# A decoder block with 32 experts: the overflow loop after the third group of experts, the first dispatch by token blocks, and one prefetch page fewer

## The chip, the cores and the metric

The kernel runs on one core of a Trainium2 chip. The time is that of the device for one execution, in microseconds (us). Three executions of the kernel before took 1099.38, 1103.64 and 1104.58; the median is 1103.64. The profile is of one more execution. The engines are TensorE (PE, with its weight loads PEld), VectorE (DVE), ScalarE (ACT), GpSimd (POOL) and SyncE (SP), which issues nearly all loads.

## The reference

The input is 512 tokens of 1024 channels. Cut to what matters here:

```python
u = rms_norm(h)
proj = u @ w_in                               # z | xBC | dt | glu_a | glu_b | two gates
y_ssd  = rms_norm(ssd(conv4(xBC)) * silu(z)) @ w_ssd_out
y_conv = silu(layer_norm(causal_dwconv31(glu_a * sigmoid(glu_b)))) @ w_conf_out
h = h + (sigmoid(gate_ssd) * y_ssd + sigmoid(gate_conv) * y_conv) @ w_o
u = rms_norm(h)
# hierarchical MoE: the best of 4 groups, then the 2 best of its 8 experts
for each expert e:                            # 32 experts, D_EXPERT = 512
    xb = the tokens that chose e
    h[those tokens] += gate * ((silu(xb @ w_gate[e]) * (xb @ w_up[e])) @ w_down[e])
h = h + (p @ w_ple_proj) * sigmoid(rms_norm(h) @ w_ple_gate)
out = rms_norm(h)
```

All values are float32. An expert has 6 MB of weights.

## The kernel before, in words

Products in the mixers and the epilogue split each float32 operand into two parts of a faster type: a high part (a cast on ACT, line 302) and the remainder (a subtraction on DVE), and multiply high by high, high by low and low by high. The names `uh` and `ul` are such halves of the activations, and `w` that of a weight.

All work is a list `units`. A unit has weight loads and a function that issues its matmuls. `step()` takes the next one: it splits the weights of the units ahead (`split`), issues loads (`pump`, line 282, on SP), runs the unit's matmuls and then what was attached to that unit: a `job` belongs to a fixed unit, while a `task` has a first and a last unit between which a credit of PE time lets it go. All weights go into a pool of `PAGES` = 11 tiles of 1 MB, tag `w`; a mixer weight takes half of one. `state["room"]` counts the half pages that may be filled, and `free(n)` adds to it. One page's place is taken in the MoE by the one-hot tables, so ten are left.

Ahead of the MoE, `mixer` units of the two branches, `w_o`, and the router follow each other. `XD` is the unit by which the SSD products are done, `NB` the first unit of the MoE. In the mixers the layer norm sums `k` tiles (ACT, line 929) with a matmul by `ones`.

The MoE has seven groups, counted from 0 here and in what follows, of 4, 5, 5, 5, 5, 5 and 3 experts. The tokens of an expert are put into slots of 32 by a one-hot matmul (`disp`, four accumulators of 16 matmuls, each with a high part `u2h` and a low part `u2l` of the activations, whose tiles are `uh` and `ul` in the traces, and a copy to `cj`). Two quads of slots then pass six units each: gate and up in two halves of the depth (`eg`, `eu`), and two of down (`ed`), 32 matmuls a unit. The result is scaled by the gate weight in two parts (the last on DVE, `bt`), and `combine` adds it to `h` (`Z` in the traces) with the transposed one-hot tables: eight steps of four matmuls and a DVE addition. The combine of a group and the dispatch of the one after the next stand as tasks among the units of a group.

An expert with more tokens than its slots is served by the overflow loop, lines 1704 and 1705: `n_ext` (tile `cd`) is loaded into a register by every engine, and the body runs so often. With these inputs it is zero. Before, the loop stands behind all seven groups and ahead of the epilogue, whose transposes (`ident`, `Z`) need the finished `h`.

Of the kernel before, what the change touches and what calls it, by code (L numbers as in the profile page):

```python
# [19 lines left out]
NT = T // 128  # L20
KD = D // 128
# [46 lines left out]

_CST = {}
PAGES = 11  # L70
BT = dict(room=8, raw=20, hi=1, page=1.27, mm=3.5, cap=5.0, sp=5, fill=[1.8, 0.9], late=[7, 2])


# [63 lines left out]
def tile_hybrid(ctx: ExitStack, tc: tile.TileContext, x, p, chan, rowv, rows, cst, w_in, w_ssd, w_conf, w_o,  # L137
# [8 lines left out]
    def st(shape, dt, tag, bufs=1):  # L146
        return sb.tile(shape, dt, name=tag, tag=tag, bufs=bufs)
# [7 lines left out]
    def mm(o, a, b, start, stop):  # L155
        nc.tensor.matmul(o, a, b, start=start, stop=stop)
        if b.dtype == F32:
            nc.pe[0] += max(0.1, 3 * o.shape[-1] / 2370)
# [67 lines left out]
    def page(shape, dt, key):  # L226
# [3 lines left out]
        if v is None:  # L230
            v = st([128, 4 * T], dt, "w", PAGES)
            pend[key] = v[:, 2 * T:]
# [23 lines left out]
    def unit(src, mms, cost=0.0, plain=False):  # L256
        srcs = [] if src is None else src if isinstance(src, list) else [src]
        units.append(dict(lds=[load(s, plain) for s in srcs], mms=mms, cost=cost, plain=plain))
        return len(units) - 1

    def job(n, f, *a):
        jobs[n].append((f, a))
# [4 lines left out]
    def task(early, late, cost, f, *a):  # L267
        tasks.append((early, late, cost, f, a))

    def pump():  # L270
        while state["load"] < len(loads):
# [4 lines left out]
            if ld["wide"]:  # L276
                state["room"] -= 2
                ld["t"] = st([128] + list(src.shape[1:]), F32, "w", PAGES)
            else:
# [8 lines left out]
    def split_hi():  # L288
        n = state["split"]
        if n >= len(units):  # L290
            return False
        u = units[n]
        if u["lds"] and not u["plain"]:
            ld = u["lds"][0]
            if "t" not in ld:
                pump()
            if "t" not in ld:
                assert n >= NB
                return False
            u["raw"] = ld["t"]  # L300
            u["wh"], u["wl"] = [page(list(u["raw"].shape), F32R, n) for _ in range(2)]
            nc.scalar.copy(u["wh"], u["raw"])  # L302
        state["split"] += 1
        return True

    def split_lo():
        n = state["lo"]
        if n >= state["split"]:
            return
        state["lo"] += 1  # L310
        u = units[n]
        if u["lds"] and not u["plain"]:
            nc.vector.tensor_sub(u["wl"], u["raw"], u["wh"])
            free(1)

    def split():
        split_hi()
        split_lo()
# [22 lines left out]
    def after(u):  # L341
# [3 lines left out]
        state["n"] = n + 1  # L345
        state["credit"] = min(state["credit"] + BT["page"] * (2 if u["plain"] else 1) * len(u["lds"]) - u["cost"], BT["cap"])
        while True:
# [7 lines left out]
    def step():  # L355
        n = state["n"]
        top = state["top"]
        if n < NB:
            while state["split"] <= min(max(n + 2, 2 * n - NB + BT["sp"]), top):
                split()  # L360
        else:
            while state["split"] <= min(top, n + (BT["hi"] if n < NC else 6)) and split_hi():
                split_lo()
        pump()
        u = units[n]
        if u["plain"]:
            ws = [ld["t"] for ld in u["lds"]]
            u["mms"](ws)
            free(2 * len(ws))
        elif u["mms"] is not None:  # L370
            u["mms"](u["wh"], u["wl"])
        after(u)

    def run(upto=None):
        while state["n"] < (len(units) if upto is None else upto):
            step()
# [517 lines left out]
    n = 0  # L894
# [11 lines left out]
    for c in range(NT):  # L906
        js.extend(chunk(c, f0 + c * TUNE["stride"]))
    XD = math.ceil(max(j[0] for j in js if j[1] in (ssd_diag, ssd_skip)))
    job(XD + 1, free, 2)
    if TUNE["first"]:  # L910
        step_jobs(js)
    for w in seq:
# [96 lines left out]
    conv_out(0)  # L1009
    job(conv_out(1), free, BT["room"] - 6)  # L1010

# [47 lines left out]
    job(NO, load_h)  # L1059
    NB = len(units)  # L1060
    for i in range(4, 0, -1):
        job(NB - i, free, 2 if i > 1 else BT["raw"] - BT["room"] - 8)

    def add_h(c, n):
        hv = hh_["h"][:, c, n * 512:(n + 1) * 512]
# [3 lines left out]
    R = {}  # L1069
# [105 lines left out]
    G = {}  # L1175

    def weights(w, b):

        if b < NFIX:
            v = w[b]  # L1180
        else:
            if b not in G:
                G[b] = nc.sync.value_load(R["eid"][0:1, b:b + 1], min_val=0, max_val=NEXP - 1)
            v = w[bass.ds(G[b], 1)].rearrange("o a n -> (o a) n")
        return v.rearrange("(p k) n -> p k n", p=128)
# [5 lines left out]
    GW = {gi: QS * len(g) for gi, g in enumerate(GROUPS)}  # L1191
# [8 lines left out]
    def gu_unit(gi, q, i, kp):  # L1200
        quad = GROUPS[gi][q]

        def mms(ws):
            if kp == 0:
                PG[gi, q, i] = acc()
            for kk in range(4):
                k = 4 * kp + kk
                strips(PG[gi, q, i], XT[gi, k // 2][:, k % 2, q * QS:(q + 1) * QS], [w[:, kk, :] for w in ws], quad,
                       k == 0, k == KD - 1)
        return unit([lambda b=m[0]: weights((eg, eu)[i], b)[:, 4 * kp:4 * kp + 4, :] for m in quad], mms, BT["mm"],  # L1210
                    True)
# [32 lines left out]
    def one_hot(gi):  # L1244
        if gi == 0:
            G["ohs"] = st([128, 2, NT, 2 * QS], F32R, "w", PAGES)
        return G["ohs"][:, gi % 2]
# [19 lines left out]
    def disp_mm(gi, kp, pt, a):  # L1267
        w = GW[gi]
        for kk in range(2):
            k = 2 * kp + kk  # L1270
            for c in range(NT):
                mm(pt[:, kk * w:(kk + 1) * w], R[("u2h", "u2l")[a]][:, c, k * 128:(k + 1) * 128],
                   G["oh", gi][:, c, :w], a == 0 and kk == 0 and c == 0, a == 1 and kk == 1 and c == NT - 1)
# [7 lines left out]
    def disp(gi, kp):  # L1281
        pt = acc()
        for a in range(2):
            disp_mm(gi, kp, pt, a)
        disp_out(gi, kp, pt)
# [50 lines left out]
        fill_pe(state["n"], room)  # L1336

    combined = NB + 4
    for gi, g in enumerate(GROUPS):
        last = gi == len(GROUPS) - 1  # L1340
        first = len(units)
        if last:
            for n in range(2):
                p_unit(n)
            job(first - 6, free, -2)
            job(first - 5, p_load)
            job(first - 5, free, -2)
            for k in range(2):
                job(first - 3 + k, p_tr, k)
            job(first - 2, free, 2)  # L1350
            job(first - 2, free, -8)
        for q in range(len(g)):
            for kp in range(2):
                for i in range(2):
                    u = gu_unit(gi, q, i, kp)
            job(u - 1, hid_act, gi, q)
            job(u, hid_mul, gi, q)
            job(u, fill_now, BT["fill"][0])
            job(u, hid_tr, gi, q)
            job(u, fill_now, BT["fill"][1])  # L1360
            if last:
                job(u - 1, free, -2)
            for f in range(2):
                u = d_unit(gi, q, f)
            task(combined, u - 1, 1.4, back, gi, q)
            if last:
                job(u - 1, free, -2)
            for n in range(2):
                job(u, y_hi, gi, q, n)
                job(u, y_lo, gi, q, n)  # L1370
        if last:
            for n in range(2):
                for c in range(NT):
                    job(u, combine, gi, c, n)
            continue
        for n in range(2):
            for c in range(NT):
                task(u + 1, u + 5, 0.23 * 2 * len(g), combine, gi, c, n)
        combined = u + 5
        o = first + (BT["late"][0] if gi == 0 else BT["late"][1])  # L1380
        for q in range(len(GROUPS[gi + 1])):
            job(o, hot, gi + 1, q)
        for kp in range(4):
            task(o + 1, u, 0.115 * 16, disp, gi + 1, kp)
    for i in range(3):
        unit(None, None)
    NC = len(units)
# [144 lines left out]
    def u2_lo(n, c):  # L1532
        t = R.pop(("g", c, n)).rearrange("t (k p) -> t k p", k=KD)
        nc.vector.scalar_tensor_tensor(half(R["u2l"], c, n), t, rs[:, c:c + 1], half(R["u2h"], c, n),
                                       op0=OP.mult, op1=OP.subtract)
# [44 lines left out]
    for c in range(NT):  # L1580
        o = pp[:, c * NEXP:(c + 1) * NEXP]
# [7 lines left out]
    for c in range(NT):  # L1589
        hot_first(c)  # L1590
    for i in range(2 * NT):
        u2_lo(i // NT, i % NT)
    N2 = 2 * NEXP


# [93 lines left out]
    for i, f in enumerate((order0, order4, order1, order2, order3, order5, order6, order7, order8)):  # L1689
        job(NB + (i + 1) // 2, f)  # L1690
    pts = [acc() for _ in range(4)]
    for a in range(2):
        for k in range(4):
            disp_mm(0, k, pts[k], a)
    for k in range(4):
        disp_out(0, k, pts[k])
        if k % 2:
            step()
            step()
    run(NC)  # L1700

    W32 = [128, NEXP]
    ext, ntot, icnt, eidf, pos, gat = (R[n] for n in ("ext", "ntot", "icnt", "eidf", "pos", "gat"))
# [1 line left out]
    with tc.For_i(0, n_ext):  # L1705
# [39 lines left out]
        oh = st([128, NT, SL], F32R, "m", 2)  # L1745
# [38 lines left out]
        for w in (eg, eu):  # L1784
            o = acc()
            for q in range(4):
                for kk, (wh, wl) in enumerate(piece(w, [128, 2, DE], 2 * q)):
                    k = 2 * q + kk
                    a = xt[:, k].rearrange("p h a s -> p (h a s)")
# [36 lines left out]
                nc.vector.tensor_add(hv, hv, po)  # L1826
        nc.vector.tensor_scalar(icnt, icnt, 1.0, None, op0=OP.add)
    banks.remove(bank)
    if dbg == "moe":
        for c in range(NT):  # L1830
            nc.sync.dma_start(out[c * 128:(c + 1) * 128, :], h[:, c, :])
        return
# [77 lines left out]
```

## Time and profile before

| | us |
|---|---|
| median of three executions | 1103.64 |
| the profiled execution, its own time | 1103.84 |
| its span | 1102.1 |
| PE busy | 1017.3 |
| DVE busy | 561.7 |
| ACT busy | 344.7 |

The mean granted clock of TensorE is 0.978. The span runs from the first instruction to the last; the execution's own time is 1.7 us longer. A start time in the rows below is counted from the start of the span. A busy PE need not be PE at its peak.

### The profile page before, as it was taken

The numbers are of one execution on the slowest core, as the hardware profiler recorded it, in microseconds if no ns is written. First come the engines' busy times: TensorE is split into PE (matmuls) and PEld (weight loads), VectorE is DVE, ScalarE is ACT, GpSimd is POOL, SyncE is SP. The second block draws the span as 40 slices with busy tenths as digits, with TensorE's granted clock in tenths as the row PEclk, the third lists the DMA queues.
The fourth block names the chain that finished last, engine by engine and source line by source line (L and its number), as shares of the span: only waits on it lengthen the run. The fifth ranks groups of instructions, "written<-read, shape, count | busy, mean of one in ns | idle before, by whom it ended". The sixth has DMA issues, their size and how long they took to land. (4 is left out here: it accounts for less than half of the span.)

```text
span 1102.1 us, 15676 instructions
## 1 busy us (share of the span) xinstructions
PE 1017.3 (92%) x6262; PEld 673.0 (61%) x6262; DVE 561.7 (51%) x1004; ACT 344.7 (31%) x646; POOL 14.7 (1%) x32
## 2 busy tenths in 40 slices
PE   5999999999989999999799998989979979889796
PEld 4788889877767877788634453433514415345385
DVE  6689998897889955563721311202103002022365
ACT  5433446766443234432411010100100100121263
POOL 1000000000000000000000000000000000000010
PEclk9999999999999999999899999999999999999899
DMA  9323222201422323356189999999999999998701
GB/s 267 95 70 102 89 78 77 77 1 41 113 77 82 110 77 115 109 195 224 40 350 388 372 387 422 420 421 421 420 421 420 420 421 421 417 401 367 284 2 76
DMA packets 95660, 255.97 MB, mean 232 GB/s; under 512 B 4784, under 2 KB 62144, under 8 KB 71008
## 3 DMA queue, kind: packets, MB, share of 16 engines
q1 hardware_dynamic: 94896, 252.73, 60.6%
q0 software_dynamic: 688, 2.22, 0.7%
q8 instruction: 50, 0.82, 0.3%
q14 instruction: 26, 0.21, 0.1%
HBM read 252.83 MB, written 2.10 MB: 231 GB/s over the span
## 5 line engine op out<-in xcount | busy, mean ns | idle before, releaser
L120 PE MATMUL acc<-uh,w 128*128 128x512 f32 x704 | 231.0, 401 | 1.7 <-DVE w L120 1.6
L120 PE MATMUL acc<-w,cj 128*32 128x512 f32 x1664 | 200.3, 599 | 13.6 <-DMA w<-eu 9.9
L120 PE MATMUL acc<-w,uh 128*128 128x256 f32 (+2 forms) x752 | 161.7, 325 | 0.9 <-DVE w L120 0.9
L120 PEld LDWEIGHTS acc<-uh,w 128*128 128x128 f32 x704 | 132.2, 188 | 32.7 <-DVE w L120 2.6
L120 PE MATMUL acc<-w,m 128*32 128x512 f32 (+1 forms) x960 | 132.3, 595 | 19.2 <-DMA w<-ed 14.5
L120 PEld LDWEIGHTS acc<-w,cj 128*32 128x32 f32 x1664 | 54.4, 110 | 137.4 <-issue 106.6
L120 PE MATMUL acc<-ul,w 128*128 128x512 f32 x352 | 137.2, 390 | 0.0
L120 DVE SCALAR_TENSOR_TENSOR cj<-glu,chan,cj 128x512 f32<-128x512 f32 x180 | 130.8, 747 | 2.2
L120 PEld LDWEIGHTS acc<-w,uh 128*128 128x128 f32 x752 | 118.4, 193 | 21.0 <-issue 10.2
L120 DVE TENSOR_TENSOR w<-w 128x1024 fp32r<-128x1024 f32 x86 | 104.6, 1221 | 43.4 <-ACT w L302 43.2
L120 PE MATMUL acc<-w,ul 128*128 128x256 f32 (+2 forms) x488 | 117.2, 307 | 0.0
L302 ACT CAST w<-w 128x1024 fp32r<-128x1024 f32 x86 | 89.6, 1052 | 67.5 <-PE acc L120 54.4
L120 PE MATMUL acc<-w 128*128 128x512 f32 x384 | 102.0, 404 | 3.1 <-ACT w L302 2.4
L120 PEld LDWEIGHTS acc<-w,m 128*32 128x32 f32 (+1 forms) x960 | 44.5, 127 | 91.2 <-issue 53.1
L120 DVE TENSOR_TENSOR k<-k,acc 128x512 f32<-128x512 f32 x21 | 19.2, 913 | 151.4 <-PE acc L120 151.4
L120 PEld LDWEIGHTS acc<-w 128*128 128x128 f32 x384 | 73.9, 194 | 22.2 <-ACT w L302 2.8
L120 DVE TENSOR_TENSOR Z<-Z,acc 128x512 f32<-128x512 f32 x64 | 43.3, 686 | 85.1 <-PE acc L120 85.1
L120 PEld LDWEIGHTS acc<-w,ul 128*128 128x128 f32 x488 | 77.2, 189 | 5.6
L120 PEld LDWEIGHTS acc<-ul,w 128*128 128x128 f32 x352 | 66.2, 188 | 15.1 <-issue 1.7
L1227 ACT ACTIVATE k<-acc 128x512 f32<-128x512 f32 x13 | 7.8, 597 | 160.9 <-PE acc L120 160.9
L120 DVE SCALAR_TENSOR_TENSOR bt<-glu,chan,bt 128x512 f32<-128x512 f32 x60 | 43.0, 748 | 0.7
L120 DVE SCALAR_TENSOR_TENSOR bt<-acc,gt,k 128x512 fp32r<-128x512 f32 x12 | 9.0, 751 | 66.8 <-ACT k L1311 66.1
(270 smaller groups left out, 885.6 us busy)
## 6 DMA issues: line engine op xcount, KB each, us to landing
w<-eg SPq DMA_DIRECT2D x64, 1024.0 KB, 13.7
w<-eu SPq DMA_DIRECT2D x64, 1024.0 KB, 14.8
w<-ed SPq DMA_DIRECT2D x64, 1024.0 KB, 15.1
w<-w_in SPq DMA_DIRECT2D x52, 512.0 KB, 5.1
w<-w_ssd_out SPq DMA_DIRECT2D x8, 512.0 KB, 5.3
w<-w_conf_out SPq DMA_DIRECT2D x8, 512.0 KB, 4.3
w<-w_o SPq DMA_DIRECT2D x8, 512.0 KB, 4.8
w<-w_ple_gate SPq DMA_DIRECT2D x8, 512.0 KB, 13.3
```

What stands on the lines that cost most here:

```text
L120: return f(*a, **k)
L302: nc.scalar.copy(u["wh"], u["raw"])
L1227: nc.scalar.activation(t, PG.pop((gi, q, 0)), AF.Silu)
```

## The change

There are three parts.

1. `LG = 3`. The units run up to the first unit of group 3, and the overflow loop stands there. The combine of group 2 becomes a job of that group's last unit. The dispatch of group 3 is no longer a task among group 2's units; it is issued behind the loop, four accumulators in a row, and then the remaining units run.
2. In the first dispatch (group 0) the low part goes token block by token block (`c` outside, `k` inside) instead of accumulator by accumulator, and the low halves are written in the same order.
3. The two half pages that were given to the pool one unit behind `XD` are given to it with the last ones, one unit ahead of `NB`.

```diff
--- before.py
+++ after.py
@@ -68,6 +68,8 @@
 
 _CST = {}
 PAGES = 11
+
+LG = 3
 BT = dict(room=8, raw=20, hi=1, page=1.27, mm=3.5, cap=5.0, sp=5, fill=[1.8, 0.9], late=[7, 2])
 
 
@@ -906,7 +908,6 @@
     for c in range(NT):
         js.extend(chunk(c, f0 + c * TUNE["stride"]))
     XD = math.ceil(max(j[0] for j in js if j[1] in (ssd_diag, ssd_skip)))
-    job(XD + 1, free, 2)
     if TUNE["first"]:
         step_jobs(js)
     for w in seq:
@@ -1059,7 +1060,7 @@
     job(NO, load_h)
     NB = len(units)
     for i in range(4, 0, -1):
-        job(NB - i, free, 2 if i > 1 else BT["raw"] - BT["room"] - 8)
+        job(NB - i, free, 2 if i > 1 else BT["raw"] - BT["room"] - 6)
 
     def add_h(c, n):
         hv = hh_["h"][:, c, n * 512:(n + 1) * 512]
@@ -1336,9 +1337,12 @@
         fill_pe(state["n"], room)
 
     combined = NB + 4
+    NL = None
     for gi, g in enumerate(GROUPS):
         last = gi == len(GROUPS) - 1
         first = len(units)
+        if gi == LG:
+            NL = first
         if last:
             for n in range(2):
                 p_unit(n)
@@ -1375,13 +1379,17 @@
             continue
         for n in range(2):
             for c in range(NT):
+                if gi == LG - 1:
+                    job(u, combine, gi, c, n)
+                    continue
                 task(u + 1, u + 5, 0.23 * 2 * len(g), combine, gi, c, n)
         combined = u + 5
         o = first + (BT["late"][0] if gi == 0 else BT["late"][1])
         for q in range(len(GROUPS[gi + 1])):
             job(o, hot, gi + 1, q)
         for kp in range(4):
-            task(o + 1, u, 0.115 * 16, disp, gi + 1, kp)
+            if gi != LG - 1:
+                task(o + 1, u, 0.115 * 16, disp, gi + 1, kp)
     for i in range(3):
         unit(None, None)
     NC = len(units)
@@ -1589,7 +1597,7 @@
     for c in range(NT):
         hot_first(c)
     for i in range(2 * NT):
-        u2_lo(i // NT, i % NT)
+        u2_lo(i % 2, i // 2)
     N2 = 2 * NEXP
 
 
@@ -1689,15 +1697,19 @@
     for i, f in enumerate((order0, order4, order1, order2, order3, order5, order6, order7, order8)):
         job(NB + (i + 1) // 2, f)
     pts = [acc() for _ in range(4)]
-    for a in range(2):
-        for k in range(4):
-            disp_mm(0, k, pts[k], a)
+    for k in range(4):
+        disp_mm(0, k, pts[k], 0)
+    w = GW[0]
+    for c in range(NT):
+        for k in range(KD):
+            mm(pts[k // 2][:, k % 2 * w:(k % 2 + 1) * w], R["u2l"][:, c, k * 128:(k + 1) * 128], G["oh", 0][:, c, :w],
+               False, c == NT - 1 and k % 2 == 1)
     for k in range(4):
         disp_out(0, k, pts[k])
         if k % 2:
             step()
             step()
-    run(NC)
+    run(NL)
 
     W32 = [128, NEXP]
     ext, ntot, icnt, eidf, pos, gat = (R[n] for n in ("ext", "ntot", "icnt", "eidf", "pos", "gat"))
@@ -1826,6 +1838,9 @@
                 nc.vector.tensor_add(hv, hv, po)
         nc.vector.tensor_scalar(icnt, icnt, 1.0, None, op0=OP.add)
     banks.remove(bank)
+    for kp in range(4):
+        disp(LG, kp)
+    run(NC)
     if dbg == "moe":
         for c in range(NT):
             nc.sync.dma_start(out[c * 128:(c + 1) * 128, :], h[:, c, :])
```

On ACT, in the mixer, the rows show the cast of a weight among the `L929` activations (`k` tiles of the layer norm). Before:

```order
L929 ACTIVATE k_3318<-cj 128x512 [waits DVE_49]
L929 ACTIVATE k_3321<-bt 128x512 [waits DVE_49,PE_49,Activation_49]
L302 CAST w<-w 128x1024 [waits DMAHW7_49,PE_49]
L929 ACTIVATE k_3350<-cj 128x512 [waits DVE_49,Activation_49]
L302 CAST w<-w 128x1024 [waits DMAHW0_49,Activation_49]
L929 ACTIVATE k_3400<-bt 128x512 [waits DVE_49]
```

And in the changed kernel, the same six:

```order
L930 ACTIVATE k_3315<-cj 128x512 [waits DVE_49]
L930 ACTIVATE k_3318<-bt 128x512 [waits DVE_49,PE_49,Activation_49]
L304 CAST w<-w 128x1024 [waits DMAHW7_49]
L930 ACTIVATE k_3347<-cj 128x512 [waits DVE_49,PE_49,Activation_49]
L304 CAST w<-w 128x1024 [waits DMAHW0_49,Activation_49]
L930 ACTIVATE k_3397<-bt 128x512 [waits DVE_49,PE_49]
```

The order of the rows stays. The cast of the third row waits for a DMA and for PE before, and for the DMA alone after.

On SP, the rows ahead of the loop before stand at the end of the MoE: the loads of `w_ple_gate`, the load of the loop's count `cd`, and the branches past the loop.

```order
L282 DMA w<-w_ple_gate 128x2x512 [waits DMAHW3_49]
L282 DMA w<-w_ple_gate 128x2x512 [waits DMAHW4_49,PE_49]
L1704 TENSOR_LOAD cd [waits DVE_49]
L1704 ISA x2
L1705 COMPARE_AND_BRANCH
L1705 UNCONDITIONAL_BRANCH [waits SP_sequencer_49,DMAHW0_49,DMAHW1_49,DMAHW2_49,DMAHW3_49,DMAHW4_49,DMAHW5_49,DMAHW6_49,DMAHW7_49]
```

In the changed kernel the same branches stand behind the loads of group 3's first pages (`eg`, `eu`):

```order
L284 DMA w<-eg 128x2048 [waits DMAHW5_49,PE_49]
L284 ISA
L284 DMA w<-eu 128x2048 [waits DMAHW6_49,PE_49]
L1716 TENSOR_LOAD cd [waits DVE_49]
L1716 ISA x2
L1717 COMPARE_AND_BRANCH
L1717 UNCONDITIONAL_BRANCH [waits SP_sequencer_49,DMAHW0_49,DMAHW1_49,DMAHW2_49,DMAHW3_49,DMAHW4_49,DMAHW5_49,DMAHW6_49,DMAHW7_49]
```

Behind the loop's body, SP's next rows are these:

```order
L284 DMA w<-eu 128x2048
L284 ISA
L284 DMA w<-ed 128x2048
L284 ISA
L284 DMA w<-ed 128x2048
L284 ISA
L284 DMA w<-ed 128x2048 [waits PE_49]
```

The loop has moved among the loads of `eu` and `ed`: seven pages of group 3 are issued ahead of it. Of the loads behind it, three wait for nothing, and the fourth waits for PE.

On PE, before, the dispatch of group 3 (`w,uh` and `w,ul` into `acc`) stands among the units of group 2 (`w,cj` and `w,m`); four of its eight rows, and the units around them:

```order
L120 MATMUL acc<-cb,w 128x32 x8
L120 MATMUL acc<-w,cj 32x512 x16
L120 MATMUL acc<-w,uh 128x256 x8
L120 MATMUL acc<-w,ul 128x256 x8
L120 MATMUL acc<-w,uh 128x256 x8
L120 MATMUL acc<-w,ul 128x256 x8
L120 MATMUL acc<-w,cj 32x512 x48
```

In the changed kernel PE has the loop's branches behind the last matmuls of combine (`bt,glu`):

```order
L122 MATMUL acc<-k_5751,glu 128x512
L122 MATMUL acc<-bt,glu 128x512
L1716 TENSOR_LOAD cd
L1717 COMPARE_AND_BRANCH
L1717 UNCONDITIONAL_BRANCH x2
```

And behind the loop's body:

```order
L1717 UNCONDITIONAL_BRANCH
L122 MATMUL acc<-w,uh 128x256 x8
L122 MATMUL acc<-w,ul 128x256 x8
L122 MATMUL acc<-w,uh 128x256 x8
L122 MATMUL acc<-w,ul 128x256 x8
L122 MATMUL acc<-w,uh 128x256 x8
L122 MATMUL acc<-w,ul 128x256 x8
L122 MATMUL acc<-w,uh 128x256 x8
L122 MATMUL acc<-w,ul 128x256 x8
L122 MATMUL acc<-w,cj 32x512 x64
```

The dispatch's 64 matmuls of group 3 have moved out of group 2 and stand between the loop and the first units of group 3, `w,cj` x64.

## Rows read from the trace of the kernel before

**Rows 1.** The page, part 1: busy us (share of span), instructions

```profile
PE 1017.3 (92%) x6262; PEld 673.0 (61%) x6262; DVE 561.7 (51%) x1004; ACT 344.7 (31%) x646; POOL 14.7 (1%) x32
```

**Rows 2.** Windows, group 3: busy (count) per engine, PEclk, DMA share, GB/s

```profile
754.98:829.99 75.01, 67.90 (x517) 29.52 (x514) 13.20 (x27) 8.42 (x14) 0.00 (x0) 0.98 1.01 421
```

**Rows 3.** Waits of PE from 620 to 1030: us in total, times, longest

```profile
PE acc L120 <- DMA w<-ed: 14.5, 13, 2.3
```

**Rows 4.** Timeline of ACT, 403 to 422: start, us, instruction [idle <-releaser]

```profile
404.41 0.63 ACT L929 ACTIVATE k<-bt 128x512 f32<-128x512 f32 x1 [0.32 <-ACT k L929]
410.10 1.04 ACT L302 CAST w<-w 128x1024 fp32r<-128x1024 f32 x1 [5.06 <-PE acc L120]
```

**Rows 5.** The page, part 5: the casts

```profile
L302 ACT CAST w<-w 128x1024 fp32r<-128x1024 f32 x86 | 89.6, 1052 | 67.5 <-PE acc L120 54.4
```

**Rows 6.** Timeline of PE, 403 to 422

```profile
407.61 0.62 PE L120 MATMUL acc<-uh,w 128*128 128x512 f32 x2
408.07 0.39 PE L120 MATMUL acc<-ul,w 128*128 128x512 f32 x1
...
413.78 1.05 PE L120 MATMUL acc<-ones,k 128*128 128x1 f32 x8 [2.93 <-ACT k L929]
414.69 4.59 PE L120 MATMUL acc<-w 128*128 128x512 f32 x12
```

**Rows 7.** Windows in the stretch of rows 6, columns as in rows 2

```profile
414.00:420.00 6.00, 6.00 (x29) 5.06 (x28) 1.83 (x2) 2.46 (x4) 0.00 (x0) 0.72 0.00 0
```

**Rows 8.** Timeline of PE, then of DVE, first dispatch

```profile
538.42 0.45 PE L120 MATMUL acc<-dtx 128*128 128x32 bf16 x10 [5.62 <-DVE dtx L120]
539.80 6.36 PE L120 MATMUL acc<-w,uh 128*128 128x256 f32 x32 [0.93 <-DVE w L120]
545.99 3.79 PE L120 MATMUL acc<-w,ul 128*128 128x256 f32 x32
...
540.57 5.38 DVE L120 SCALAR_TENSOR_TENSOR ul<-cj,rst,uh 128x512 fp32r<-128x512 f32 x8
```

**Rows 9.** Waits of SP's queue, 1015 to 1043; windows there

```profile
SPq L1705 <- SPq L1705: 9.2, 5, 4.0
...
1037.00:1038.00 1.00, 1.00 (x6) 0.84 (x5) 1.00 (x3) 0.00 (x0) 0.00 (x0) 1.00 0.11 43
```

**Rows 10.** Timeline of PE, end of group 2 and start of group 3

```profile
750.09 4.56 PE L120 MATMUL acc<-w,m 128*32 128x512 f32 x25 [1.44 <-DMA w<-ed]
...
764.40 3.64 PE L120 MATMUL acc<-w,cj 128*32 128x512 f32 x32
```

**Rows 11.** Timeline of DVE, end of group 2 and the combine

```profile
754.98 1.61 DVE L120 SCALAR_TENSOR_TENSOR bt<-acc,gt,k 128x512 fp32r<-128x512 f32 x2 [15.02 <-ACT k L1311]
759.85 0.69 DVE L120 TENSOR_TENSOR Z<-Z,acc 128x512 f32<-128x512 f32 x1 [3.26 <-PE acc L120]
760.79 0.69 DVE L120 TENSOR_TENSOR Z<-Z,acc 128x512 f32<-128x512 f32 x1 [0.25 <-PE acc L120]
```

**Rows 12.** Timeline of SP where the stream restarts; windows there

```profile
553.38 0.80 SPq L282 DMA_DIRECT2D w<-ed  x2
...
554.20:554.60 0.40, 0.40 (x8) 0.13 (x4) 0.33 (x3) 0.00 (x0) 0.00 (x0) 1.00 1.72 246
```

**Rows 13.** Timelines of PE and DVE at the loop's exit; a window there

```profile
1042.42 3.15 PE L120 MATMUL acc<-ident,Z 128*128 128x128 f32 x16 [3.53 <-DVEq L1705]
...
1047.01 0.40 PE L120 MATMUL acc<-w,ul 128*128 128x512 f32 x1
...
1035.91 4.86 DVE L120 TENSOR_TENSOR Z<-Z,acc 128x512 f32<-128x512 f32 x8
1040.69 1.22 DVE L120 TENSOR_TENSOR w<-w 128x1024 fp32r<-128x1024 f32 x1
...
1045.91 0.74 DVE L120 SCALAR_TENSOR_TENSOR ul<-acc,chan,uh 128x512 fp32r<-128x512 f32 x1
...
1043.00:1044.00 1.00, 1.00 (x7) 1.00 (x6) 0.06 (x1) 0.89 (x2) 0.31 (x1) 0.51 0.53 109
```

## Prediction

> **What bounds the kernel now.** I read the page's busy shares first: PE is busy for 1017.3 us of a span of 1102.1 [rows 1], so the kernel looks like a TensorE kernel from end to end. The windows by expert group say otherwise for the long middle. Between the ends of two groups lie 75.01 us, in which PE has 67.90 us of work, while the DMA engines are busy all the time (share 1.01) at 421 GB/s [rows 2]. A group is 30 pages of 1.049 MB, so a page takes 1.049 MB / 421 GB/s = 2.49 us, and 30 of them 74.7 us: the groups follow the weight stream. The list of PE's waits in this part is led by `ed` pages that have not landed [rows 3]. So there are two regimes. Until about 553 us, where the stream of expert weights is let go, the time of PE's chain is the time of the kernel; from there on to the last `ed` page an idle microsecond of the DMA queue is a microsecond of the end, whereas PE can lose some 7 us per group (75.01 - 67.90) for nothing. Behind the last page the chain is PE and DVE again.
>
> The sum below is made against the profiled execution, 1103.84 us (span 1102.1 and 1.7 around it); the median of the runs shown, 1103.64, is 0.2 lower.
>
> **The buffer change.** Two half pages stay in the pool for longer. Where the prefetch in the mixer took the last free page, it no longer does: in the order of ACT, the cast between the `L929` activations waits for DMA and PE before, and for DMA alone after. In the trace this cast is the place where PE stops. ACT is done at 404.41 + 0.63 = 405.04, but its cast starts only at 410.10, after 5.06 us of waiting for PE, which still reads the page [rows 4]; the kernel's 86 casts wait 54.4 us for PE in all [rows 5]. PE finishes its unit, and then stands for 2.93 us until ACT gives it the next `k` [rows 6]. With the page free the cast can start at 405.04, five microseconds earlier, and the 2.93 us go. With the stop goes what follows it: the 12 matmuls from 414.69 take 4.59 us, the granted clock of that stretch being 0.72 [rows 6, 7]. At full speed such matmuls start 0.23 us apart (two of them from 407.61 to 408.07), so 12 take 11 x 0.23 + 0.4 = 2.9: 1.7 us less. Together -4.6, with the bounds 0 (another wait takes the same place) and -5.06 (all that the cast waited). Late next is the DVE half of the split, which follows the cast. That one page less is prefetched I cost at nothing, since SP's order keeps its loads several units of work ahead. The gain comes before the stream of expert weights is let go, so it shifts all that follows.
>
> **The first dispatch.** 64 matmuls stay 64. Their low half now goes by token blocks, so that each `ul` block is used when both its halves are written. In the trace the high part ends at 545.99 and DVE writes the eight `ul` tiles until 540.57 + 5.38 = 545.95 [rows 8]: the low part could not start much earlier for PE, and does not wait for DVE. Now the four accumulators finish together, so that the copies to `cj` come in one row at the end instead of one after another; the next unit needs the first. I take -0.2, with -0.5 and +0.5 as bounds; where `ul` now arrives in the wanted order, nothing else is late.
>
> **The loop in the middle.** The loop makes no trip here, but its exit is a meeting point. On SP the branch past the loop stands behind the weight loads and waits for all eight hardware DMA lanes, and every other engine waits at the exit for SP. The trace of before shows the price of that wait at the end of the kernel: SP spends 9.2 us at the loop on its own waits, and the DMA share falls to 0.11 in 1037 to 1038 before the loop is left [rows 9]. There it was hidden: nothing was left to load, and DVE was still adding. In the new place it meets a full queue. SP's order has seven pages of group 3 in front of the loop and three free pages behind it.
>
> In the time of before, the last `ed` of group 2 lands at 750.09, which is where PE's wait for it ends [rows 10], and the seven pages behind it land at 750.09 + 7 x 2.49 = 767.5. Combine is no cover for this: it can start when DVE has the last `bt`, 754.98 + 1.61 = 756.6, and its eight steps are 0.93 us apart, as two adds on DVE show, 759.85 and 760.79 [rows 11], so that DVE is done at about 764.7. So SP sets the exit: 767.5, and about half a microsecond for branches, 768.0. The stream starts again after that. After an issue at 553.38 the first traffic is seen in 554.2 to 554.6 [rows 12], so 0.8 us at least: the DMA engines stand from 767.5 to 769.2 or so, with the ramp 1.9 us.
>
> Then only three pages can be filled, 3 x 2.49 = 7.5 us, to 776.7. The next page comes free when PE has run a unit, and PE has the moved dispatch of group 3 in front of its units, since it is now issued behind the loop. That is 64 matmuls of 128x256, just what the first dispatch is, and after an idle of 3.3 us (764.7 to 768.0). The first dispatch also follows a pause, of 5.62, and its first 32 matmuls take 6.36 us against 3.79 for the next 32; all 64 take 545.99 + 3.79 - 539.80 = 10.0 [rows 8]. So 768.1 + 10.0 = 778.1, a unit of 32 matmuls 3.64 [rows 10], 781.7; issue to traffic 0.8, 782.5. The queue stands a second time, for 5.8 us. Sum +7.7. Bounds: 0, if the exit does not wait for the queue (at the end of before it cost the stream nothing), and +11.3, if the first unit behind the dispatch runs at half speed too (3.6 more). Between them I take the worked value, since each of its terms has a row.
>
> PE does not add to it. After the loop it has, for group 3, 67.9 less the combine (8 x 0.93 = 7.4), 60.5 us, so it could be done at 838.6; the stream would let it end at 829.99 + 7.7 = 837.7. The microsecond between them is given back in the next group, which has 7 us of room.
>
> The Trainium skill, page "DMA: Bandwidth & Descriptors", section "Anatomy of one DMA — SWDGE (gpsimd) path", puts a fixed cost of about 2.0 us on each DMA, most of it the receipt of the last write, and speaks of the software path. The trace shows about 0.8 us to first traffic on the hardware queue [rows 12]; by the page's figure each of the two restarts would be up to 1.2 us longer, and the sum up to 2.4 higher. No run so far separates the receipt; the row decides.
>
> **The loop away from the end.** The transposes of the epilogue start at 1042.42, after PE has stood for 3.53 us at the loop's exit; then the granted clock is at 0.51, the lower level of 1.2 GHz [rows 13]. Without the exit they could follow the adds. But DVE is late next: eight adds until 1035.91 + 4.86 = 1040.77, then a split 1.22, a `ul` 0.74, a split 1.22 and the second `ul` 0.74, so 1044.7, where before it is 1045.91 + 0.74 = 1046.65 [rows 13]. That `ul` is what PE reads at 1047.01. So -2.0. Bounds: -0.5 (DVE's adds come late because combine shares the engine with the splits), and -5.1, which is the idle 3.53 and half of the transposes' 3.15.
>
> **Sum.** -4.6 - 0.2 + 7.7 - 2.0 = +0.9 on 1103.84, so 1104.7; on the footing of the median 1104.5.
>
> **The rivals.**
> The drain is hidden (17%). The engines pass a loop without trips, and the weights queued before it go on landing beside it. For it: in before the exit held no transfer up. Against it: SP's 9.2 us. Then only the sequence combine, dispatch is left, which PE's 7 us of room hold, and -4.6 - 0.2 - 2.0 = -6.8 gives 1096.8.
>
> The mixer's gain is not there (14%). Another cast or PE's next `k` waits at the same place, since of the 54.4 us that casts wait for PE this one is only 5.06 [rows 5]. The loop's price stays: 1104.5 + 4.6 = 1109.1, on the border of slower.
>
> PE does not get its clock back behind the loop (11%). This is the slower side, and its place is the moved dispatch. If the clock stays low through the whole of the 64 matmuls, because PE starts against weights that come in pieces, they cost twice what the first dispatch's fast half does, 4 x 3.79 = 15.2 instead of 10.0, and the unit behind it 3.6 more. The page comes free 8.8 us later with the queue empty: 1113.3. It decides when the dispatch behind the loop takes over 13 us. Against it: the first dispatch recovered within its first 32 matmuls.
>
> **How the numbers follow.** The forecast has 58%, its own range being 1101 to 1108.5 from the bounds of the loop's price and of the end. A change of 0.5%, 5.5 us, is about what can be told from none: 1098.1 to 1109.2. All of the forecast and half of the second rival lie in it, less a little for each side: same 0.63. The drain hidden is faster, with a little of the forecast's edge, 0.18; the clock and the other half of the mixer rival are slower, 0.19. The range that leaves two in ten out is 1097.5 to 1110.5.
>
> **What would show it.** Steps right: no wait of PE near 410 and a clock near 1 there; at the end of group 2, near 750 to 764 us in the new time, a stop of SP at the loop of 13 us or more, a DMA share near zero twice, for 2 and for 6 us, the second until the first unit behind the dispatch ends; group 4's end about 3 us later than before (7.7 - 4.8), and no wait for the loop ahead of the transposes. Wrong: a DMA share that stays at 1.0 around the loop, or a single gap; group ends that do not shift together; a wait of 2 us or more for ACT that stays in the mixer.

## The result, and the profile after

| | us, median | range | ratio to before, 95% interval |
|---|---|---|---|
| before, the executions of the comparison | 1102.12 | 1099.38 to 1104.58 | |
| changed | 1108.84 | 1106.82 to 1111.52 | 1.0063 (1.0045 to 1.0082) |

The change makes the kernel 6.7 us slower, 0.63%. The forecast was 1104.5, no change that can be told. The time lies in the range of 1097.5 to 1110.5, but above the forecast's own range, which ended at 1108.5: what took it in was room that had been left for rivals. The sum had +0.9 on the profiled execution, where the two profiled executions differ by 1108.81 - 1103.84 = +5.0. Most mechanisms were the right ones; the price of one was far too low, and one was missing. The profile shows it in the order of the forecast's parts.

**The mixer.** PE in the changed kernel, at the place of [rows 6]: start, us, instructions.

```profile
409.76 1.84 PE L122 MATMUL acc<-ones,k 128*128 128x1 f32 x16
411.46 2.99 PE L122 MATMUL acc<-w 128*128 128x512 f32 x12
```

```profile
414.00:420.00 6.00, 5.73 (x33) 4.54 (x32) 3.46 (x15) 2.33 (x2) 0.00 (x0) 1.00 0.60 205
```

The wait of 2.93 us for `k` is gone, sixteen `ones` products run in one piece, and the 12 matmuls behind them take 2.99 us where they took 4.59. The window answers to [rows 7]: the granted clock is 1.00 where it was 0.72. The `ones` group behind those started at 419.12 before and starts at 414.29 now: 4.8 us.

**The first dispatch**, as in [rows 8].

```profile
534.96 7.11 PE L122 MATMUL acc<-w,uh 128*128 128x256 f32 x32 [0.94 <-DVE w L122]
541.91 3.93 PE L122 MATMUL acc<-w,ul 128*128 128x256 f32 x32
```

The shift of 4.84 us at its start is kept, but the first 32 matmuls take 7.11 instead of 6.36, so the 64 end 3.9 us earlier, not 4.8. DVE's last rows of group 0 come at 604.76 against 610.35, 5.6 us earlier: nothing of that is left there.

**The loop.** SP waits, in the stretch 700 to 800 (total, times, longest), and SP's issues (start, us to the last of the row, loads):

```profile
SPq L1717 <- SPq L1717: 18.6, 7, 3.7
```

```profile
742.50 21.43 SPq L284 DMA_DIRECT2D w<-eu  x2
764.17 12.55 SPq L284 DMA_DIRECT2D w<-ed  x4
...
783.30 3.75 SPq L284 DMA_DIRECT2D w<-eu  x3
797.71 0.91 SPq L284 DMA_DIRECT2D w<-eg  x2
```

SP waits at the loop seven times, 18.6 us in all: one wait for each page that is on its way. The first `eu` page goes out at 742.50, and the other of that row, as the end of the row says, only at about 763.6, behind the loop. Of the four `ed` two go out at once and two when a page comes free.

Windows of 2 us around it, with the columns of [rows 2], the last three being the granted clock, the DMA share and GB/s:

```profile
758.00:760.00 2.00, 0.00 (x0) 0.00 (x0) 0.00 (x0) 0.00 (x0) 0.00 (x0) 0.97 0.92 377
760.00:762.00 2.00, 0.00 (x0) 0.00 (x0) 0.00 (x0) 0.00 (x0) 0.00 (x0) 0.50 0.18 74
762.00:764.00 2.00, 1.01 (x4) 1.01 (x5) 1.23 (x5) 0.00 (x0) 0.00 (x0) 0.50 0.06 16
764.00:766.00 2.00, 2.00 (x11) 2.00 (x11) 0.27 (x2) 0.00 (x0) 0.00 (x0) 0.50 0.70 164
...
772.00:774.00 2.00, 2.00 (x23) 0.68 (x25) 0.00 (x0) 0.58 (x1) 0.00 (x0) 1.00 0.34 143
774.00:776.00 2.00, 2.00 (x24) 0.58 (x20) 0.00 (x0) 0.00 (x0) 0.00 (x0) 1.00 0.03 8
776.00:778.00 2.00, 2.00 (x24) 0.65 (x20) 0.00 (x0) 0.00 (x0) 0.00 (x0) 1.00 0.58 123
...
796.00:798.00 2.00, 2.00 (x19) 0.65 (x12) 0.00 (x0) 0.00 (x0) 0.00 (x0) 1.00 0.67 279
798.00:800.00 2.00, 2.00 (x23) 1.37 (x26) 0.62 (x4) 0.59 (x1) 0.00 (x0) 1.00 0.54 152
```

These are three gaps in a stream that before ran at 421 GB/s throughout. What a window lost is 2 us x (1 - its GB/s / 421). The first gap, 758 to 766, has lost 0.2 + 1.6 + 1.9 + 1.2 = 5.0 us; the second, 772 to 778, 1.3 + 2.0 + 1.4 = 4.7; the third, 796 to 800, 0.7 + 1.3 = 2.0. With 0.2 in the window at 804 and 0.7 in those from 810 to 814 the sum is 12.5 (windows that lost less than 0.12 are left out). The forecast had two gaps of 1.9 and 5.8.

PE in that stretch, answering to [rows 10]:

```profile
744.91 3.62 PE L122 MATMUL acc<-w,m 128*32 128x512 f32 x26 [1.44 <-DMA w<-ed]
...
762.99 2.08 PE L122 MATMUL acc<-w,uh 128*128 128x256 f32 x8 [6.74 <-SPq L1717]
...
772.18 13.94 PE L122 MATMUL acc<-w,cj 128*32 128x512 f32 x128
786.05 1.21 PE L122 MATMUL acc<-w,uh 128*128 128x256 f32 x8
```

The last `ed` of group 2 has landed at 744.91, 5.2 us earlier than before. Combine follows without the next group's first unit in between, and ends at 756.3, sooner than the forecast had it (764.7 - 4.8 = 759.9); so PE stands for 6.74 us at the loop and not for 3.3, which costs nothing, since SP sets the exit. PE is let out of the loop at 762.99, does the dispatch of group 3, then four units in one piece, and from 786.05 on the whole dispatch of group 4 in one piece too, until 794.0: during that no page comes free, SP's `eu` row ends at 787.05, and its next `eg` goes out at 797.71, which is the third gap. The last `ed` of group 3 lands 9.2 us later than before, where the forecast had 7.7 - 4.8 = 2.9. First the changed kernel, then the kernel before:

```profile
834.24 3.19 PE L122 MATMUL acc<-w,m 128*32 128x512 f32 x25 [1.44 <-DMA w<-ed]
```

```profile
825.03 4.64 PE L120 MATMUL acc<-w,m 128*32 128x512 f32 x25 [1.44 <-DMA w<-ed]
```

**The end**, PE and DVE where [rows 13] had them.

```profile
1044.82 1.91 PE L122 MATMUL acc<-ident,Z 128*128 128x128 f32 x16
...
1050.46 0.80 PE L122 MATMUL acc<-w,ul 128*128 128x512 f32 x1 [0.83 <-DVE ul L122]
```

```profile
1041.95 4.86 DVE L122 TENSOR_TENSOR Z<-Z,acc 128x512 f32<-128x512 f32 x8
...
1049.66 0.74 DVE L122 SCALAR_TENSOR_TENSOR ul<-acc,chan,uh 128x512 fp32r<-128x512 f32 x1
```

The transposes follow the combine without a wait, and PE then waits for DVE's `w` and `ul`, as was said: the second `ul` is written at 1049.66 + 0.74 = 1050.40, 3.75 us later than before, whereas the eight adds start 6.04 us later than before. So this part gains 2.3 us up to there; 1.0 us of it is left at the end of the span.

### The profile page after: what moved, and what is told of

Same layout as the page of the kernel before. It is cut to its first block, busy times and chain, and to the rows that moved or that the text cites. A ratio compares the mean times of both kernels' runs of the same rounds, so it can differ in the third digit from the quotient of the medians.

```text
span 1107.1 us, 15679 instructions
## 1 busy us (share of the span) xinstructions
PE 1013.9 (92%) x6262; PEld 671.9 (61%) x6262; DVE 561.5 (51%) x1004; ACT 344.4 (31%) x646; POOL 14.5 (1%) x32
## 5 line engine op out<-in xcount | busy, mean ns | idle before, releaser
L122 PE MATMUL acc<-w,m 128*32 128x512 f32 (+1 forms) x960 | 128.1, 575 | 21.8 <-DMA w<-ed 16.4
L1279 ACT COPY cj<-acc 128x512 f32<-128x512 f32 (+1 forms) x28 | 15.3, 558 | 87.3 <-PE acc L122 87.3
## 6 DMA issues: line engine op xcount, KB each, us to landing
w<-eg SPq DMA_DIRECT2D x64, 1024.0 KB, 13.3
w<-eu SPq DMA_DIRECT2D x64, 1024.0 KB, 13.3
```

Of the source, the lines that this page charges most:

```text
L122: return f(*a, **k)
L1279: nc.scalar.copy(t, pt[:, :2 * w].rearrange("p (k s) -> p k s", k=2))
```

## The experiments

Each ratio is to the kernel before, timed beside it: its median was 1101.34 beside e1 to e4 and 1101.74 beside e5 to e8. A "lost" time is summed over the 2 us windows from the last `ed` of group 2 to that of group 3 as above, in one profiled execution.

| label | the kernel | median | ratio (95%) | lost, us |
|---|---|---|---|---|
| changed | loop moved, dispatch, buffer | 1108.84 | 1.0063 (1.0045 to 1.0082) | 12.5 |
| e1_buffer | before + buffer change | 1096.06 | 0.9956 (0.9938 to 0.9974) | |
| e2_loop | before + loop move | 1114.07 | 1.0116 (1.0097 to 1.0136) | 13.3 |
| e3_noloop | changed, no loop at all | 1100.11 | 0.9997 (0.9977 to 1.0016) | 6.0 |
| e4_bufdisp | before + buffer + dispatch | 1095.80 | 0.9943 (0.9926 to 0.9961) | 0.0 |
| e5_dispfirst | changed, dispatch of group 3 ahead of the loop | 1102.61 | 1.0006 (0.9991 to 1.0022) | 7.6 |
| e6_dispspread | changed, that dispatch spread in group 2 | 1099.74 | 0.9980 (0.9967 to 0.9993) | 5.4 |
| e7_noloop_end | e4, no loop at all | 1095.47 | 0.9933 (0.9913 to 0.9953) | |
| e8_drain | e4 + one wait of SP alone | 1101.32 | 0.9994 (0.9981 to 1.0007) | 5.2 |

**The parts alone.** e1 is the kernel before with

```diff
-    job(XD + 1, free, 2)
...
-        job(NB - i, free, 2 if i > 1 else BT["raw"] - BT["room"] - 8)
+        job(NB - i, free, 2 if i > 1 else BT["raw"] - BT["room"] - 6)
```

> The kernel before with the buffer change alone. Theory (the stop in the mixer goes and the gain shifts all that follows): PE has no wait of 2.9 us near 410, the expert stream starts 4.8 us earlier, and the time is 4 to 5 us below that of before, ratio 0.9955 to 0.9965. Rival (the gain is taken back when one prefetch page fewer is there at the start of the experts): the last weight page lands at the same time as before, ratio 0.999 to 1.001.

Measured: 0.9956, 4.8 us by the ratio and 5.3 by the medians. PE has no stop in the mixer, and its first dispatch starts 5.8 us earlier than before, at 534.01 against 539.80 (1.1 us of it stand already ahead of that place):

```profile
410.52 2.99 PE L120 MATMUL acc<-w 128*128 128x512 f32 x12
...
534.01 6.99 PE L120 MATMUL acc<-w,uh 128*128 128x256 f32 x32 [0.93 <-DVE w L120]
```

The gain of the mixer reaches the end; the rival is out.

e2 has the diff of the change without this and without the two edits of the first dispatch.

> The kernel before with the move of the loop alone (the first dispatch and the buffers as before). Theory (the drained weight queue, read in the changed kernel as gaps of 5.0, 4.7 and 2.1 us and 14.4 us between the last down pages of groups 2 and 3, with some 1.6 us given back later and 1.0 gained at the end): 11 to 13 us above before, ratio 1.010 to 1.012. Rival (the loop costs the 7.7 us of the forecast, less 2.0 at the end, and another part of the change costs the rest): 5 to 6 us above, ratio 1.005.

Measured: 1.0116, 12.7 us by the medians. PE's stop of 2.93 us in the mixer is there as before, and the stream loses 13.3 us around the loop. So the loop's move alone costs more than twice the 7.7 - 2.0 = 5.7 of the forecast.

e4 has e1's edits and the two of the first dispatch.

> The kernel before with the buffer change and the first dispatch by token blocks, the loop left at the end. Theory: the buffer's gain of 4.8 us, and for the dispatch between -0.2 (the forecast) and +1.0 (what the start of the stream in the changed kernel shows): 1.0 us or less apart from the buffer change alone, ratio to before 0.9955 to 0.997.

Measured: 1095.8, 0.3 below e1, which is less than the two intervals can tell. So the dispatch's order is worth nothing that can be measured here. e4 has the lowest median of the versions that leave nothing out, not to be told from e1's, and beats both kernels.

**Without the loop.** e3 takes the loop and its body out of the changed kernel:

```diff
-    n_ext = nc.values_load(ntot, min_val=0, max_val=T * 2 // SL + NEXP)
-    with tc.For_i(0, n_ext):
-        ...
```

> The changed kernel without the overflow loop (it leaves out the service of overflowing experts, which makes no trip with these inputs); the combine of group 2 and the dispatch of group 3 stay where the change put them, one behind the other. Theory (the meeting point at the loop drains the queue): the DMA share stays at 1.0 from group 2 to group 3, and the time falls by 12 to 15 us against the changed kernel, to 0.994 to 0.996 of before. Rival (PE's order, combine and then dispatch in one piece with no page coming free, starves the queue): the gaps stay, and the time falls by under 4 us, to a ratio of 1.002 or more.

Measured: 0.9997, 8.7 us below the changed kernel by the medians and 7.3 by the ratios. Both theories are half right. Windows of e3, columns as above:

```profile
764.00:766.00 2.00, 2.00 (x20) 0.52 (x16) 0.00 (x0) 0.54 (x1) 0.00 (x0) 1.00 0.92 381
766.00:768.00 2.00, 2.00 (x24) 0.65 (x20) 0.00 (x0) 0.00 (x0) 0.00 (x0) 1.00 0.36 152
768.00:770.00 2.00, 2.00 (x24) 0.65 (x20) 0.00 (x0) 0.00 (x0) 0.00 (x0) 1.00 0.77 188
...
788.00:790.00 2.00, 2.00 (x23) 0.87 (x11) 0.00 (x0) 0.04 (x1) 0.00 (x0) 1.00 0.57 229
790.00:792.00 2.00, 2.00 (x19) 1.09 (x23) 0.62 (x4) 0.54 (x1) 0.00 (x0) 1.00 0.73 197
```

The gap that began at 758 is gone, but two others are there, which lose 2.6 and 2.0; with smaller ones behind them it is 6.0. PE and SP show why:

```profile
756.49 1.08 PE L122 MATMUL acc<-w,uh 128*128 128x256 f32 x8
...
763.84 13.94 PE L122 MATMUL acc<-w,cj 128*32 128x512 f32 x128
```

```profile
748.73 19.69 SPq L284 DMA_DIRECT2D w<-ed  x4
```

PE's combine runs up to 756.49, the dispatch follows until 763.8, and the first unit ends some 3.6 us later, at 767.4. SP issues the first two of these four `ed` pages near 749 and 750, and then all ten pages are taken; the other two wait until 767.5. Ten pages behind a last landing at 745.3 are 24.9 us, so the tenth lands near 770.2, but the rate falls before that, and the next issue comes too late to fill it. I had reckoned these 15 us of PE as held by PE's room of 7 us a group. But what covers the stream is not PE's room; it is the free pages, and PE gives none back in that time.

**Where the dispatch stands.** e5 moves it ahead of the loop, behind the combine:

```diff
+    for kp in range(4):
+        disp(LG, kp)
     with tc.For_i(0, n_ext):
         ...
-    for kp in range(4):
-        disp(LG, kp)
```

> The changed kernel with the dispatch of group 3 in front of the loop, behind the combine (the loop's body, which makes no trip, leaves out the casts and subtractions of its weights, whose tiles are taken by that dispatch). Theory (the second gap is the dispatch that stands between the restart and the first page that comes free): the first gap of 5 us stays, the second, 4.7 us, goes, and the time falls by 4 to 6 us against the changed kernel. Rival (SP's three free pages set the second gap, whatever PE does): it stays, and the time is within 1.5 us of the changed kernel.

Measured: 6.2 us below the changed kernel by the medians (1108.84 and 1102.61) and 6.3 by the ratios, a little more than expected. Windows, and SP's waits at the loop:

```profile
762.00:764.00 2.00, 2.00 (x21) 2.00 (x20) 0.00 (x0) 0.77 (x2) 0.00 (x0) 1.00 0.24 94
764.00:766.00 2.00, 1.51 (x14) 1.31 (x12) 0.00 (x0) 0.77 (x2) 0.00 (x0) 1.00 0.04 16
766.00:768.00 2.00, 0.38 (x4) 0.16 (x8) 1.40 (x5) 0.14 (x1) 0.00 (x0) 0.97 0.03 8
768.00:770.00 2.00, 2.00 (x16) 0.49 (x12) 0.10 (x1) 0.00 (x0) 0.00 (x0) 0.50 0.88 242
770.00:772.00 2.00, 2.00 (x20) 0.60 (x16) 0.00 (x0) 0.00 (x0) 0.00 (x0) 0.67 0.96 360
```

```profile
SPq L1719 <- SPq L1719: 20.1, 7, 4.0
```

There is one gap and then a full stream (up to 806, where 0.5 is lost), so the second gap is indeed the dispatch between the restart and the next free page; the rival, three pages whatever PE does, falls. The one gap has lost 6.6 us in 762 to 772, more than 5.0: SP's seventh wait, the one of 4.0 us, ends only at 765.8, where a page every 2.49 us would have it at 746.9 + 7 x 2.49 = 764.3, and PE's first unit starts at 767.62. Why that page came 1.5 us late was not tried.

e6 spreads it over group 2 as a task again:

```diff
-            if gi != LG - 1:
-                task(o + 1, u, 0.115 * 16, disp, gi + 1, kp)
+            task(o + 1, u, 0.115 * 16, disp, gi + 1, kp)
```

and takes out the four calls behind the loop.

> The changed kernel with the dispatch of group 3 as tasks among group 2's units, as before the change (body of the loop as in the run beside it). Theory: only the first gap is left, 4 to 5 us, and with the two later ones gone the time is 6 to 8 us below the changed kernel, at a ratio to before of 0.999 to 1.001. Rival (the loop stops PE too, and what PE loses there cannot be made up): no better than the dispatch in front of the loop.

Measured: 0.998, 9.1 us below the changed kernel, a little more than expected. The windows have the first gap and no other:

```profile
758.00:760.00 2.00, 0.00 (x0) 0.00 (x0) 0.00 (x0) 0.00 (x0) 0.00 (x0) 0.95 0.80 328
760.00:762.00 2.00, 0.00 (x0) 0.00 (x0) 0.00 (x0) 0.00 (x0) 0.00 (x0) 0.50 0.10 41
762.00:764.00 2.00, 1.22 (x8) 0.40 (x12) 1.37 (x5) 0.00 (x0) 0.00 (x0) 0.50 0.00 0
764.00:766.00 2.00, 2.00 (x12) 0.39 (x8) 0.13 (x1) 0.00 (x0) 0.00 (x0) 0.50 0.70 172
```

They have lost 0.4 + 1.8 + 2.0 + 1.2 = 5.4 us. PE stands for 6.66 us at the loop in this kernel and makes it up, so the rival falls too. The dispatch of group 4 stands in one piece here as well (778.54 to 786.45) and in e5 (783.19 to 791.12), and the windows there are full. By itself, then, that piece does not make the third gap. In e6 SP has issued 11 pages between the restart and its pause at 779.55; in the changed kernel it is 8 between the restart behind the second gap, at 775.9, and the pause at 787.05, and the pauses are equally long, 10.6 and 10.7 us. So the third gap follows from the second.

**A drain by itself.** e8 is e4, with one line after the seventh page of group 3 has been issued:

```diff
+            if state["load"] == G["drain"]:
+                nc.sync.dma_start(st([1, 8], F32, "xs"), ld["t"][0:1, 0, 0:8])
```

> The kernel before with the buffer change and the first dispatch by token blocks, and one drain put in by hand: behind the seventh page of group 3, SP issues a copy of 32 bytes out of that page, so that it waits until the page has landed before it issues the next load; no other engine waits. Theory (a drained queue loses from the landing of its last page to the landing of the next, beyond a page's 2.5 us, what issue and completion take): 2.5 to 4.0 us above the kernel without the copy, 1095.8. Forecast's term: 1.9. Rival (the loss is that of the meeting of all engines, and a drain by itself costs nothing): within 0.8 us.

Measured: 1101.32 against 1095.8, +5.5 us, above even the theory's range. SP's issues and the windows:

```profile
762.84 0.81 SPq L287 DMA_DIRECT2D xs<-w  x1
...
764.52 2.20 SPq L284 DMA_DIRECT2D w<-ed  x4
```

```profile
760.00:762.00 2.00, 2.00 (x20) 0.53 (x18) 0.65 (x1) 0.00 (x0) 0.00 (x0) 1.00 0.30 123
762.00:764.00 2.00, 2.00 (x19) 0.75 (x12) 0.00 (x0) 0.00 (x0) 0.00 (x0) 1.00 0.01 4
764.00:766.00 2.00, 2.00 (x15) 1.15 (x17) 1.09 (x2) 0.00 (x0) 0.00 (x0) 1.00 0.58 98
```

SP issues the small copy once the page has landed, then the next pages without a further wait for PE, and the stream still has a gap of 0.3 + 1.4 + 2.0 + 1.5 = 5.2 us (0.3 in 758 to 760). No other engine is made to wait for SP in this kernel, and PE's clock is at 1.00 throughout. So the first gap does not need the meeting of the engines, nor a lower clock of PE. It is not the empty queue alone either: from the landing to the next page's issue SP takes 1.1 us here (762.84 to 763.92, most of it the issue of the copy) and 1.4 us at the loop of the changed kernel (762.2 to 763.6). By an estimate from these rows some 4 us are left in both for a queue that runs dry and fills again.

**The loop at the end.** e7 takes the loop out of e4.

> The kernel before with the buffer change and the first dispatch by token blocks, and without the overflow loop (it leaves out the service of overflowing experts, which makes no trip with these inputs). Against the same kernel with the loop at the end, 1095.8, this shows what the loop costs there. Forecast's term: 2.0 us, so 1093.8. What the changed kernel's shifts show: 1.0, so 1094.8. Rival (all of the wait of 3.5 us and the slow clock behind it): 5 us, so 1090.8.

Measured: 0.3 below e4, with an interval of 2 us to either side, so the times can't tell 0 from 2. The spans of the two profiles, 1095.3 and 1093.4, differ by 1.9 us. From the start of the eight adds to the second `ul` e4 takes 10.7 us and e7 8.5, a gain of 2.3 as in the changed kernel, and PE in e7 waits for DVE as forecast:

```profile
1032.16 1.91 PE L120 MATMUL acc<-ident,Z 128*128 128x128 f32 x16
...
1037.85 0.50 PE L120 MATMUL acc<-w,ul 128*128 128x512 f32 x1 [0.83 <-DVE ul L120]
```

What the loop costs at the end is about 0 to 2 us, and the rival with 5 is out.

**The sum of the runs.** The lost time agrees with what each kernel is above e4, by the ratios: 5.2 lost and (0.9994 - 0.9943) x 1101.7 = 5.6 above for e8, 6.0 and 5.9 for e3, 5.4 and 4.1 for e6, 7.6 and 6.9 for e5, 12.5 and 13.2 for the changed kernel (each pair agrees within the intervals, some 2 us to either side). e2 without the mixer's gain has 13.3 and 12.8 above before. To within those 2 us, what the stream loses here is what the kernel loses.

## Why the prediction was right or wrong

- **What bounds the kernel: right.** A microsecond of the stream is one of the end, as the table says to within some 2 us, and in the mixer a microsecond of PE is.
- **The buffer change, -4.6: right.** -4.8 in the trace, -4.8 to -5.3 in the times of e1.
- **The first dispatch, -0.2: right in size, and empty.** e4 and e1 differ by 0.3. In the profiled execution of the changed kernel the dispatch itself took 0.9 longer, which was gone by the end of group 0. Most of that is not due to the new order: in e1, with the old one, the first 32 matmuls take 6.99.
- **The loop, +7.7: the mechanism right, the size wrong.** Three terms make it up. The step that failed is this: "so 0.8 us at least: the DMA engines stand from 767.5 to 769.2 or so, with the ramp 1.9 us". The time of the last landing was right: seven pages of 2.49 us behind 744.91 give 762.3, and SP's seventh wait ends at 762.2. But the rate falls from 758 on, as the last pages' packets thin out, and the last of them are seen near 761.5: 1.9 us are lost by 762, where the forecast had the queue full. The issue comes at 763.6, 1.4 us behind that wait, where half a microsecond was reckoned for branches; the first traffic comes at 764.4, 0.8 behind it as forecast, and full rate is back only at 766. That is 5.0 lost instead of 1.9, 5.2 in e8 and 5.4 in e6. What I took from the row of the restart was the start of the first packet. The better number stood ready in the landings of the kernel before: of the two pages of that very row [rows 12], the first, issued at 553.38 into an empty queue, takes 4.9 us to its landing, and the first page behind the gap in the changed kernel 5.0,

```profile
w<-ed SPq DMA_DIRECT2D x1, 1024.0 KB, 4.9
```

```profile
w<-eu SPq DMA_DIRECT2D x1, 1024.0 KB, 5.0
```

where in the running stream a page lands every 2.49. The forecast's 1.9 counted nothing of the falling end and only 0.2 of the slow beginning. The Trainium skill, "DMA: Bandwidth & Descriptors", section "Anatomy of one DMA — SWDGE (gpsimd) path", has about 2.0 us of fixed cost for each DMA; the forecast weighed it and chose the row of 0.8. By an estimate from that figure of the Trainium skill the sum would have given up to 1106.9, nearer to 1108.84 and still short of it. That section of the Trainium skill speaks of the software path; on the hardware queue of this trace some 0.7 us pass from the last packet (761.5) to the end of SP's wait (762.2), and 0.8 from the issue to the first traffic, 1.5 together.
- The second gap was forecast at 5.8 and is 4.7; e5 shows that the dispatch behind the loop makes it.
- The third gap, 2.0, was not forecast. "PE does not add to it" was wrong for the queue: PE's own time was indeed given back, but a dispatch in one piece frees no page, and where the queue has had a gap shortly before, as here, the stream starves once more. e3 shows this without any loop, and e5 and e6 show that the same piece costs nothing where the second gap is absent.
- **The loop away from the end, -2.0: right, within what could be seen.** 2.3 at the second `ul`, 1.0 at the end of the span, 1.9 between the spans of e4 and e7. The times alone can't tell it from nothing.
- **The sum.** With the first gap at 5.0, the second at 4.7, the third at 2.0 and 0.9 besides, the loop is +12.5, above even the forecast's bound of +11.3, and the sum -4.6 - 0.2 + 12.5 - 2.0 = +5.7. The profiled executions differ by +5.0 and the medians by +6.7.
- **The rivals.** A drain that is hidden: out, by e8. A mixer without its gain: out, by e1. A clock that does not come back behind the loop: out; the dispatch there took 9.2 us (762.99 to 772.18), below the 10.0 reckoned. The 6.7 us come from none of the three, but from a term of the forecast that was priced too low. Nor would a hidden drain have left the rest for nothing, as that rival had it: e3 has no drain, and combine and dispatch in one piece cost its stream 6.0 us. The time is below the prediction's border of 1109.2 for "same", which had a chance of 0.63, by 0.4 us; the interval, 1.0045 to 1.0082, says that the kernel is slower, and that the border held is in part luck.

## What to carry to other kernels

In a part bound by weight transfers, whatever makes the issuing queue wait for all that is on its way (a loop that makes no trip, or a copy of 32 bytes that reads the newest page) cost some 5 us of stream here, more than the 0.8 us to the first packet suggests; price it from the last full window to the next full window. What covers the stream is free buffers and not idle time of the computing engine, so work that frees none belongs between units that do. And of a change in several parts, run each alone: here one part was worth 5 us and another cost 13.

## What the runs showed of the hardware that was not expected

SP's wait for everything on its way is seen page by page, seven waits for seven pages of 1 MB. And a branch of PE past the loop's body took 5.0 us in the profiled execution of the changed kernel (min/median/max in ns, first and last start):

```profile
L1717 PEldq COMPARE_BRANCH  x3: 101/192/5001, 752.6 to 762.7; - x3
```

In the kernel before, the longest of PE's branches at the loop took 325 ns. The long one is no accident of one execution: in e2, which has the same loop in the same place, the longest takes 4641 ns. It began at 756.4 and ended at 761.4, ahead of the seventh page's landing at 762.2, and so did not decide when the loop was left; in e5 and e6, whose loop body leaves out some casts and subtractions, the longest takes 393 ns, and e6 has the same gap. Its cause was not tried.
